# A mixture-of-experts encoder layer: sixteen short expert turns instead of fourteen, expert 0's rows by products, rank results by plain loads

## The chip, the core and the metric

The kernel runs on one core of a Trainium2 chip. The metric is the device time of one execution in microseconds, as the median of several runs; a profiled execution gives the trace. TensorE (PE) multiplies, with its own weight loads (PEld); VectorE (DVE), ScalarE (ACT) and GpSimd (POOL) work on tiles in SBUF; SyncE (SP) only issues transfers here. Sixteen DMA engines move the data, for the queues of SP (q1) and POOL (q0) alike.

## The reference, cut

One layer over 512 tokens of width 1024: attention, a LayerNorm, then a routed mixture of experts and a last LayerNorm. All numbers are float32.

```python
h = layer_norm(DN_ALPHA * h + mix, ln1_g, ln1_b)          # after two attentions and their projections
logits = t @ w_router + b_router                          # t: 512 x 1024, 32 experts
top_v, top_i = lax.top_k(logits, 4)
top_w = softmax(top_v)
# every expert takes the tokens that chose it (2048 token-expert pairs in all):
g = minimum(xb @ w_gate[e] + b_gate[e], 7)                # w_gate[e], w_up[e], w_down[e]: 1024 x 1024
u = clip(xb @ w_up[e] + b_up[e], -7, 7)
ys = (g * sigmoid(1.702 * g) * (u + 1)) @ w_down[e] + b_down[e]
out = segment_sum(ys * row_w, row_tok)                    # the four results of a token, weighted and added
h = layer_norm(DN_ALPHA * h + out, ln2_g, ln2_b)
```

An expert's three matrices are 12 MB; all 32 experts' are 384 MB, and each is read once.

## The kernel before, in words

**Stages.** First come the LayerNorm, both attentions and the output projection. They end in the loop over four token tiles `t` in which `mix`, `norm`, `z_turn`, `route` and `places` work out the normed rows, the four experts of each token and its place in each expert's list (`posp`). The scaled rows (`affine`) go to DRAM as `h1d`. Then 32 turns follow, one expert each.

**Turns.** Experts 0 and 1 are turns 0 and 1, whatever their number of tokens. The other 30 are sorted by that number: `count`, a comparison of all counts (`cmp_`, `rank`), a one-hot matrix `atT`, and in `turns_known` the list `turnI`, from which SyncE reads the expert of each turn before it loads the turn's weights. The smallest go to the turns with `SMALL[e]`, which have 64 places (turns 2, 4, ..., 28: fourteen); the others have 128. If an expert has more tokens than its turn has places, the rest is done in a loop behind the program (`n_over`), which is skipped otherwise.

- A turn of 128 places (`products`) multiplies in fp32r: each half megabyte of weights is split by ACT (`wh`, L88) and VectorE (`wl`, L89), and `mm3` (L158) makes three products of it.
- A turn of 64 places (`products64`, L1046) multiplies in fp32 with the weights as they come, 64 columns of PE for each half of the matrix; nothing is split.

**Rows of an expert.** POOL (for experts 0 and 1 VectorE, in `places`) makes `hots`, a one-hot matrix of a token tile against the places. `choose` multiplies it with `aux` on PE, which gives each place's token, weight and rank, as `tokI`, `wgt` and `dstI`. `gather` fetches the rows from `h1d` by an indirect DMA, and `x_turn` transposes them into `XT`. For experts 0 and 1 an early `choose` gives the tokens alone (`tok0`).

**The order of the turns** is written out by hand, and each engine runs its instructions in that order: `gates_of(f)`, `ups_of(f)`, then the down products of `e = f - 1`. The functions in the tables `at` are put in front of the half megabyte with that number (0 to 7) of a product.

**Loads.** `Stream` holds a list of chunks of 1 MB and a list of slots, 14 in the expert stage. A chunk is loaded by SyncE as soon as a slot is free, in the order of the list: for each turn four chunks of gate, four of up and four of down of the turn before. A slot comes free when its chunk has been split (128 places) or multiplied (64 places).

**Results.** A result row is written to `Y` in DRAM by an indirect DMA, to the place (rank of the expert among the token's four, token). Turns 30 and 31 don't write: `last_result` keeps their results as two parts, and `last_add` adds them per token tile by products with one-hot matrices (`last_turn`) into PSUM (`lastP`). `acc` holds the residual rows. After turn 29, twelve DMAs of POOL's queue add ranks 0 to 2 of `Y` to `acc` while they move (`add_rank`, L1151); the last four follow after VectorE has added `lastP`. Then ln2's rows are loaded, and VectorE, ACT and POOL make the last LayerNorm (`row_stats`, `ln_scale`, `ln2_norm`, `ln2_affine`).

Of the kernel before, what the change touches and what calls it, by code (L numbers as in the profile page):

```python
# [37 lines left out]
C_ID, C_IE, C_KB, C_RK, C_CAP, C_P, C_PM, C_IH, C_END = 0, 128, 160, 192, 224, 256, 257, 259, 260  # L38


SMALL = {e: 2 <= e < NE - 2 and e % 2 == 0 for e in range(NE)} | {"o": False}
# [3 lines left out]
class Stream:  # L45
# [3 lines left out]
    def __init__(self, nc, look):  # L49
        self.nc, self.look = nc, look  # L50
        self.free, self.chunks, self.halves, self.live = [], [], [], {}
        self.loaded = self.split = 0
        self.limit, self.low, self.queue = 1 << 30, nc.vector, nc.sync

# [3 lines left out]
    def add(self, shape, load, halves):  # L58

        first = len(self.halves)  # L60
        self.chunks.append([shape, load, None, None])
        for n, (view, make) in enumerate(halves):
            self.halves.append((len(self.chunks) - 1, view, make, n == len(halves) - 1))
# [50 lines left out]
def hybrid_attention_moe(ctx: ExitStack, tc: tile.TileContext, x, ln0_g, ln0_b, w_in, a_sink, b_q_norm, b_k_norm,  # L114
# [94 lines left out]
    def expert_at(e):  # L209

        if e < 2:
# [6 lines left out]
    def expert_chunks(w, e):  # L218

        r = []  # L220
        for c in range(4):
            def load(raw, c=c):
                v = w[0, ds(expert_at(e), 1)]
                if SMALL[e]:
                    v = v[:, c // 2 * 512:c // 2 * 512 + 512].rearrange("a (p b) f -> (a p) b f", b=4)
                    v = v[:, c % 2 * 2:c % 2 * 2 + 2]
                else:
                    v = v.rearrange("a (p j) f -> (a p) j f", j=8)[:, 2 * c:2 * c + 2]
                st.queue.dma_start(raw, v)
            r += st.add((2, DM), load, [(lambda q, i=i: q[:, i:i + 1], None if SMALL[e] else hl((1, DM)))  # L230
                                        for i in range(2)])
# [58 lines left out]
    cols = hd.tile([128, 4, 8], F32, name="cols")  # L290
    st.low = nc.gpsimd
    for t0 in (0, 2):
# [8 lines left out]
        if t0 == 0:  # L301
            p = ps.tile([128, 32], F32, name="pp", bufs=2)
            nc.tensor.transpose(p, rows, ident[:32, :32])
            nc.vector.tensor_copy(cols, p.rearrange("p (a b) -> p a b", b=8))
    st.limit = h_av[1]
# [200 lines left out]

    Y = dram.tile([4 * T, DM], F32, name="Y")
# [262 lines left out]
    def places(t):  # L770
# [4 lines left out]
        for e in range(2):  # L775
            find(hots[e], posp[:, :, e], [t], nc.vector)
# [32 lines left out]
    hots = {e: hots_of(None, n=e) for e in range(2)}  # L809
# [12 lines left out]
    selectors(iota_e, 0, 2)  # L822
# [40 lines left out]
    route(2)  # L863
    affine(3)
    z_turn(3)
    places(2)
    route(3)
    places(3)
    st.limit = 1 << 30

    close(ps, hd)
# [3 lines left out]
    mp = pool("mp")  # L875
    ps = pool("pm", space=PSUM)
# [23 lines left out]
    tok0 = ax.tile([128, 2], I32, name="tok0")  # L900
# [5 lines left out]
    def choose(e0, n, early=False):  # L906

        c = 2 if early else 6
# [5 lines left out]
        if early:  # L914
            tokens_of(tok0[:, e0:e0 + n], q)
# [522 lines left out]
```

## Time and profile before

| | |
|---|---|
| median of three runs | 1503.54 us (1502.82 to 1511.2) |
| the profiled execution | 1502.89 us, span 1501.1 us |
| PE, busy | 1394.7 us, 93% of the span |
| VectorE, ACT, POOL, busy | 945.5, 765.9 and 252.7 us |
| DMA | 469.69 MB, 313 GB/s over the span |
| granted TensorE clock, mean | 0.972 |

Times in rows are microseconds from the start of the span. The busy slices cut the span in 40 parts, each digit tenths of a slice. PEclk is the granted share of TensorE's clock; the five engines of a stretch are PE, PEld, DVE, ACT and POOL. In a timeline, consecutive instructions of one kind are one row with their count, and a bracket gives the idle time before and what ended it. `L` numbers are lines of the kernel.

### The profile page before, as it was taken

Reading aid. Unit: us, or ns where it says so; the run is one execution under the profiler, and the core shown is the slowest. Engines: PE = TensorE matmul, PEld = TensorE weight load, DVE = VectorE, ACT = ScalarE, POOL = GpSimd, SP = SyncE. Lnnn points to the kernel's source line nnn. Section 1 sums busy time; section 2 is a strip of 40 time slices with the busy share of each in tenths; the row PEclk is TensorE's granted clock in tenths of the full one; section 3 lists DMA queues with packets and bytes.
Section 4 is the critical chain, followed back from the end, with each engine's and each line's share of the span. In section 5 each row is a group of like instructions: output and inputs, shape, how many; then the busy total and the mean of one; then the engine's idle time right before and its main releaser. Section 6 shows DMA issues by size and latency. Waiting matters only on the chain.

```text
span 1501.1 us, 19430 instructions
## 1 busy us (share of the span) xinstructions
PE 1394.7 (93%) x6885; PEld 967.1 (64%) x6885; DVE 945.5 (63%) x1444; ACT 765.9 (51%) x1064; POOL 252.7 (17%) x295
## 2 busy tenths in 40 slices
PE   5999999999679999999799999999999999999990
PEld 3778877888557656475555756657566474667870
DVE  6675666464779548384754845747446383567986
ACT  4555556542357546264354635636446273556861
POOL 2000430101540210102021011110210101110113
PEclk9999999999799999999899999999999999999995
DMA  7362210326278999999899999999999999999996
GB/s 233 119 246 66 68 45 30 96 88 280 87 264 302 396 411 420 395 415 395 334 405 420 419 420 418 420 420 417 418 414 414 408 416 411 414 414 408 409 204 156
DMA packets 90023, 469.69 MB, mean 313 GB/s; under 512 B 10738, under 2 KB 29346, under 8 KB 40769
## 3 DMA queue, kind: packets, MB, share of 16 engines
q1 hardware_dynamic: 75888, 426.80, 70.9%
q0 software_dynamic: 13680, 41.45, 8.9%
q8 instruction: 56, 0.92, 0.2%
q14 instruction: 47, 0.38, 0.1%
q10 hardware_dynamic: 352, 0.15, 0.0%
HBM read 452.76 MB, written 24.64 MB: 318 GB/s over the span
## 4 chain that ended last, share of the span: by engine, by line
PE 41%; DMA 24%; DVE 5%; ACT 1%; issue 1%; POOL 1%; SPq 0%; ACTq 0%; DVEq 0%; POOLq 0%
PE d L158 9%; DMA raw<-in_w_down_dram 9%; PE g L158 8%; DMA raw<-in_w_gate_dram 8%; PE u L158 7%; PE g L1046 4%; PE u L1046 4%; PE d L1046 4%; DMA acc<-Y 3%; DMA raw<-in_w_up_dram 3%; DVE wl L89 2%; PE t L937 2%; ACT wh L88 1%; DMA Y<-y,dstI 1%; PE t L1108 1%
## 5 line engine op out<-in xcount | busy, mean ns | idle before, releaser
L89 DVE TENSOR_TENSOR wl<-raw,wh 128x1024 fp32r<-128x1024 f32 x472 | 565.3, 1227 | 122.9 <-ACT wh L88 108.9
L88 ACT ACTIVATE wh<-raw 128x1024 fp32r<-128x1024 f32 x476 | 494.6, 1057 | 183.7 <-PE d L158 63.7
L929 POOL DMA_INDIRECT xg<-h1d,tokI x30 | 42.6, 1421 | 729.2 <-PE t L1108 359.5
L153 DVE TENSOR_TENSOR atl<-t,ath 128x512 fp32r<-128x512 f32 x34 | 23.5, 690 | 178.3 <-ACT ath L152 178.0
L158 PE MATMUL d<-wh,ath 128*128 128x512 f32 x272 | 111.8, 411 | 7.2 <-ACT wh L88 7.2
L158 PE MATMUL u<-wl,xth 128*128 128x512 f32 x272 | 107.6, 395 | 8.1 <-DVE wl L89 8.1
L158 PE MATMUL g<-wh,xth 128*128 128x512 f32 x288 | 114.7, 398 | 0.0
L158 PE MATMUL d<-wl,ath 128*128 128x512 f32 x272 | 108.0, 397 | 6.8 <-DVE wl L89 6.6
L158 PE MATMUL g<-wh,xtl 128*128 128x512 f32 x288 | 112.7, 391 | 0.0
L158 PE MATMUL g<-wl,xth 128*128 128x512 f32 x288 | 112.6, 391 | 0.0
L158 PE MATMUL u<-wh,xth 128*128 128x512 f32 x272 | 108.2, 398 | 0.0
L158 PE MATMUL u<-wh,xtl 128*128 128x512 f32 x272 | 107.5, 395 | 0.0
L158 PE MATMUL d<-wh,atl 128*128 128x512 f32 x272 | 107.3, 394 | 0.0
L1046 PE MATMUL g<-raw,xth 128*64 128x512 f32 x448 | 105.4, 602 | 0.0
L1046 PE MATMUL u<-raw,xth 128*64 128x512 f32 x448 | 103.9, 600 | 0.7 <-DMA raw<-in_w_up_dram 0.7
L1046 PE MATMUL d<-raw,ath 128*64 128x512 f32 x448 | 102.8, 600 | 0.0
L158 PEld LDWEIGHTS d<-wh,ath 128*128 128x128 f32 x272 | 51.5, 189 | 28.1 <-ACT wh L88 12.4
L158 PE MATMUL pp<-hTH,wh 128*128 128x512 f32 x160 | 64.9, 406 | 0.0
L158 PEld LDWEIGHTS d<-wl,ath 128*128 128x128 f32 x272 | 51.7, 190 | 20.5 <-DVE wl L89 11.3
L1046 PEld LDWEIGHTS d<-raw,ath 128*64 128x64 f32 x448 | 29.7, 137 | 54.6 <-issue 47.9
L158 PEld LDWEIGHTS u<-wl,xth 128*128 128x128 f32 x272 | 51.9, 191 | 19.4 <-DVE wl L89 8.5
L1046 PEld LDWEIGHTS u<-raw,xth 128*64 128x64 f32 x448 | 29.0, 136 | 54.0 <-issue 47.5
(408 smaller groups left out, 2394.3 us busy)
## 6 DMA issues: line engine op xcount, KB each, us to landing
raw<-in_w_gate_dram SPq DMA_DIRECT2D x128, 1024.0 KB
raw<-in_w_down_dram SPq DMA_DIRECT2D x128, 1024.0 KB
raw<-in_w_up_dram SPq DMA_DIRECT2D x125, 1024.0 KB
raw<-in_w_in_dram SPq DMA_DIRECT2D x14, 1024.0 KB
Y<-u POOLq DMA_DIRECT2D x4, 2048.0 KB, 17.2
acc<-Y POOLq DMA_DIRECT2D x16, 512.0 KB, 10.0
raw<-in_w_out_dram SPq DMA_DIRECT2D x4, 1024.0 KB
raw<-in_w_up_dram POOLq DMA_DIRECT2D x3, 1024.0 KB, 7.6
```

Source lines behind the costliest of these rows:

```text
L88: self.nc.scalar.activation(h, src, AF.Copy)
L89: self.low.tensor_tensor(l, src, h.bitcast(F32), op=OP.subtract)
L153: nc.vector.tensor_tensor(l, src, h.bitcast(F32), op=OP.subtract)
L158: nc.tensor.matmul(o, a, b, start=start and i == 0, stop=stop and i == 2, **kw)
L929: nc.gpsimd.indirect_dma_start(out=x_[:, :T] if small else x_, out_offset=None, in_=src, in_offset=bass.IndirectOffsetOnAxis(ap=tok, axis= ...
L937: nc.tensor.transpose(p[:, j], src[:, 4 * i + j::8], ident)
L1046: nc.tensor.matmul(o[64 * i:64 * i + 64], xt(j), w[:, 0, i * 512:i * 512 + 512], start=j == 0 and sel is None, stop=j == 7, skip_group_che ...
L1108: nc.tensor.transpose(p[:, b], src[:, b:T:4], ident)
```

## The change

- **Turns.** Sixteen turns have 64 places: 1, 2, 4, ..., 24, 27, 30 and 31. Only expert 0 has a fixed turn; the other 31 are sorted.
- **Expert 0's rows** are not gathered. `pick` multiplies the normed rows of each token tile with expert 0's one-hot matrix (`hot0`) into PSUM as soon as the tile's places are known; ACT and VectorE scale the result with ln1's values (`cols1`), and it is split into `XT[0]`. Expert 0's gate and up chunks are laid out to fit. `hots` of experts 0 and 1 are now made by POOL, from the places by turn, and turn 1's rows are gathered in `first_rows`.
- **Loads.** Expert 0's down chunks stand before expert 1's gate chunks in the list. As turn 1 has an expert that is not known beforehand, `Stream.known` holds the loads there until `turns_known`. Behind the last weights come one chunk with ln2's rows and eight chunks of `Y`, two token tiles of one rank each.
- **Results.** No DMA adds in the regular program. `add_chunk` takes a chunk of `Y`, and VectorE adds its two tiles to `acc`. Turns 30 and 31 have one result tile each; `last_add` makes one fp32 product for each token tile and half.

The diff, cut:

```diff
-SMALL = {e: 2 <= e < NE - 2 and e % 2 == 0 for e in range(NE)} | {"o": False}
+SMALL = {e: e in (1, 27, 30, 31) or 2 <= e <= 24 and e % 2 == 0 for e in range(NE)} | {"o": False}
...
-        while self.loaded < len(self.chunks) and self.free:
+        while self.loaded < min(len(self.chunks), self.known) and self.free:
...
-        if e < 2:
+        if e == 0:
             return e
...
+                elif e == 0 and w is not w_down:
+                    v = v.rearrange("a (j p) f -> p (a j) f", p=128)[:, 2 * c:2 * c + 2]
...
         if e < NE:
+            if e == 1:
+                down0 = len(st.chunks)
+                expert_chunks(w_down, 0, ahead=True)
+                st.known = len(st.chunks)
             HG[e] = expert_chunks(w_gate, e)
             HU[e] = expert_chunks(w_up, e)
         if e > 0:
-            HD_[e - 1] = expert_chunks(w_down, e - 1)
+            HD_[e - 1] = expert_chunks(w_down, e - 1, behind=down0 if e == 1 else None)
+    def load_gb(raw):
+        for i, v in enumerate((ln2_g, ln2_b)):
+            nc.sync.dma_start(raw[:, i], v.to_broadcast([128, DM]))
+
+    def load_rank(r, q):
+        src = Y[r * T + q * 256:r * T + q * 256 + 256].rearrange("(a p) d -> p a d", p=128)
+        return lambda raw: nc.sync.dma_start(raw, src)
+
+    h_g2 = st.add((2, DM), load_gb, [(lambda q: q, None)])[0]
+    h_rank = {(r, q): st.add((2, DM), load_rank(r, q), [(lambda v: v, None)])[0] for q in range(2) for r in range(4)}
...
-        for e in range(2):
-            find(hots[e], posp[:, :, e], [t], nc.vector)
+        nc.vector.tensor_scalar(hot0[:, t], cnt1, posp[:, t, 0:1], None, op0=OP.is_equal)
+
+    def pick(t, first, last):
+
+        for k in range(KT):
+            nc.tensor.matmul(zp[k // 4][:, k % 4], z[t][k // 4][:, k % 4 * 128:k % 4 * 128 + 128], hot0[:, t],
+                             start=first and k % 4 == 0, stop=last, skip_group_check=True)
...
     route(2)
+    zp = [ps.tile([128, 4, 128], F32, name="s", bufs=3) for _ in range(2)]
+    pick(0, True, False)
+    pick(1, False, False)
     affine(3)
     z_turn(3)
     places(2)
+    pick(2, False, False)
     route(3)
     places(3)
+    pick(3, False, True)
...
+    XT = {0: turned("xth", "xtl")}
+    for i in range(2):
+        f = mp.tile([128, T], F32, name="rT").rearrange("p (a b) -> p a b", a=4)
+        for j in range(4):
+            g, b = (cols1[:, c, 4 * i + j:4 * i + j + 1] for c in range(2))
+            if j % 2:
+                nc.vector.tensor_scalar(f[:, j], zp[i][:, j], g, b, op0=OP.mult, op1=OP.add)
+            else:
+                nc.scalar.activation(f[:, j], zp[i][:, j], AF.Identity, bias=b, scale=g)
+        split_to(XT[0][0][:, 4 * i:4 * i + 4], XT[0][1][:, 4 * i:4 * i + 4], f)
...
-    choose(0, 1, True)
-    gather(xg, tok0[:, 0:1])
     st.queue = nc.gpsimd
     st.slots(mp, 3)
     st.load()
     st.queue = nc.sync
-    choose(1, 1, True)
...
-        selectors(turns, 2, NE)
+        selectors(turns, 1, NE)
+        st.known = 1 << 30
+        st.load()
...
+    def add_chunk(r, q):
+
+        v = st.get(h_rank[r, q])
+        for t in (2 * q, 2 * q + 1):
+            nc.vector.tensor_tensor(acc[:, t], acc[:, t], v[:, t % 2], op=OP.add)
+        st.done(h_rank[r, q])
...
     def last_result(e):
-        y = lastY[e] = slot(F32R)
-        w = wgt[:, e:e + 1]
-        for i in range(2):
-            s = slice(i * 512, i * 512 + 512)
-            nc.scalar.activation(y[:, 0, s], PD[e][i], AF.Copy, scale=w)
-            nc.vector.scalar_tensor_tensor(y[:, 1, s], PD[e][i], w, y[:, 0, s].bitcast(F32), op0=OP.mult,
-                                           op1=OP.subtract)
+        lastY[e] = mp.tile([128, T], F32, name="y" if e % 2 else "sg")
+        nc.scalar.activation(lastY[e], PD[e], AF.Copy, scale=wgt[:, e:e + 1])
...
+            s = slice(64 * i, 64 * i + 64)
+            nc.tensor.matmul(lastP[t, i], lastT[e % 2][s, t], lastY[e][s], start=e == NE - 2, stop=stop)
...
-    gates_of(0, {1: [turns_known], 2: [places_by_turn], 3: [weights_by_turn], 4: [parts_by_turn],
-                 5: [lambda: choose(0, 2), lambda: start(2, 1)]})
-    ups_of(0, {1: [lambda: choose(2, 1)], 2: [lambda: start(3, 2)], 4: [lambda: choose(3, 2)], 5: [lambda: x_turn(1, 0)], 6: [lambda: x_turn(1, 1)]})
+    def first_rows():
+        choose(0, 2)
+        gather(xg, tokI[:, 1:2], SMALL[1])
+        start(2, 1)
+
+    gates_of(0, {1: [turns_known], 2: [places_by_turn], 3: [lambda: start(0, 2), weights_by_turn], 4: [parts_by_turn],
+                 6: [first_rows]})
+    ups_of(0, {1: [lambda: choose(2, 1)], 2: [lambda: start(3, 2)], 4: [lambda: choose(3, 2)], 6: [lambda: x_turn(1, 0)]})
...
             if e == NE - 2:
-                at = {5: [lambda: a_turn(f, 0)], 6: [lambda: a_turn(f, 1)]}
+                at = {3: [lambda: add_chunk(0, 0)], 5: [lambda: a_turn(f, 0)], 6: [lambda: add_chunk(1, 0)]}
             if e >= NE - 3:
                 at[2] = [lambda: last_turn(f)]
         else:
-            at = {j + 3: [lambda t=j: last_add(e - 1, t)] for j in range(3)}
+            at = {2 * j + 1: [lambda t=j: last_add(e - 1, t)] for j in range(3)}
+            for j, c in enumerate(((2, 0), (3, 0), (0, 1), (1, 1))):
+                at[2 * j] = [lambda c=c: add_chunk(*c)]
...
-        if e == NE - 3:
-            for r in range(3):
-                for t in range(NT):
-                    add_rank(r, t, Y)
-
-    last_result(NE - 1)
+    add_chunk(2, 1)
+    add_chunk(3, 1)
+    gb = st.get(h_g2)
...
         for i in range(2):
             a = two(acc[:, t])[i]
             nc.vector.tensor_tensor(a, a, lastP[t, i], op=OP.add)
-        add_rank(3, t, Y)
-    for i, v in enumerate((ln2_g, ln2_b)):
-        nc.gpsimd.dma_start(gb[:, i], v.to_broadcast([128, DM]))
```

## Rows read from the trace of the kernel before

**Rows 1.** The page: busy slices, and median landing times of DMA issues.

```profile
DMA  7362210326278999999899999999999999999996
...
raw<-in_w_up_dram POOLq DMA_DIRECT2D x3, 1024.0 KB, 7.6
```

**Rows 2.** Stretches: us, five engines' busy time (count), PEclk, DMA share, GB/s.

```profile
457.00:900.00 443.00, 434.10 (x1967) 270.31 (x1966) 276.15 (x341) 225.92 (x264) 64.88 (x84) 0.99 0.98 397
...
900.00:1410.00 510.00, 495.91 (x2263) 317.14 (x2262) 310.46 (x348) 271.72 (x316) 70.29 (x84) 1.00 1.01 415
...
720.00:750.00 30.00, 21.90 (x86) 14.70 (x85) 21.72 (x40) 9.05 (x11) 0.00 (x0) 0.83 0.78 311
...
302.00:306.00 4.00, 4.00 (x19) 3.22 (x18) 2.12 (x3) 0.93 (x2) 0.00 (x0) 1.00 0.80 262
...
342.00:350.00 8.00, 8.00 (x36) 6.52 (x35) 2.08 (x3) 2.75 (x3) 0.00 (x0) 1.00 1.01 424
...
1440.00:1480.00 40.00, 26.38 (x116) 20.61 (x114) 28.15 (x42) 16.26 (x22) 9.70 (x12) 0.87 0.97 195
```

**Rows 3.** The chain that ended last: start us, us, what.

```profile
805.49 4.44 PE d L1046 x20
...
813.76 4.44 PE g L1046 x20
...
822.79 3.58 PE u L1046 x16
...
830.24 7.04 PE d L158 x30
...
865.60 4.44 PE d L1046 x20
...
962.35 21.69 DMA raw<-in_w_gate_dram
...
1304.70 21.68 DMA raw<-in_w_down_dram
...
1471.88 8.54 DMA acc<-Y
```

**Rows 4.** Timeline of the SyncE queue: start us, us, line, operation, count.

```profile
462.87 9.04 SPq L229 DMA_DIRECT2D raw<-in_w_up_dram  x4
...
1401.28 19.12 SPq L229 DMA_DIRECT2D raw<-in_w_down_dram  x8
```

**Rows 5.** Timelines of PE, VectorE and POOL around turn 0.

```profile
399.16 1.11 PE L740 MATMUL pp<-con,ga 128*128 128x128 f32 x4 [2.17 <-ACT ga L731]
...
416.92 0.63 PE L158 MATMUL g<-wh,xth 128*128 128x512 f32 x1
...
455.40 0.40 PE L1061 MATMUL g<-bgu,es 128*128 128x512 f32 x1
...
413.85 0.29 DVE L997 TENSOR_TENSOR lh<-lh,ew 128x128 f32<-128x128 f32 x1
...
420.80 0.17 DVE L1004 CAST turnI<-turns 1x32 int32<-1x32 f32 x1
...
433.30 5.70 POOL L768 TENSOR_SCALAR hots<-to,posp 128x128 bf16<-128x128 bf16 x4 [15.28 <-PE t L881]
...
442.30 4.92 POOL L768 TENSOR_SCALAR hots<-to,posp 128x128 bf16<-128x128 bf16 x4
```

**Rows 6.** Timeline of VectorE in the tail.

```profile
1470.30 1.28 DVE L1305 TENSOR_TENSOR acc<-acc,g 128x512 f32<-128x512 f32 x2 [1.20 <-DMA acc<-Y]
...
1480.44 1.29 DVE L267 BATCH_NORM_STATS2 bst<-acc 128x6 f32<-128x512 f32 x2 [0.84 <-DMA acc<-Y]
...
1481.76 0.21 DVE L268 BATCH_NORM_AGGREGATE mv<-bst 128x2 f32<-128x12 f32 x1
...
1483.31 7.96 DVE L1294 TENSOR_TENSOR raw<-raw,raw 128x512 f32<-128x512 f32 x6
```

**Rows 7.** Costliest groups: count, busy us, mean ns, idle before.

```profile
L89 DVE TENSOR_TENSOR wl<-raw,wh 128x1024 fp32r<-128x1024 f32 x472 | 565.3, 1227 | 122.9 <-ACT wh L88 108.9
```

More of the change, by code (lines that the diff above doesn't have):

```diff
@@ L53, in __init__ @@
         self.limit, self.low, self.queue = 1 << 30, nc.vector, nc.sync
+        self.known = 1 << 30
     def slots(self, pool, n):
@@ L216, in expert_at, with expert_chunks @@
         return turn_regs[e]
-    def expert_chunks(w, e):
+    def expert_chunks(w, e, ahead=False, behind=None):
         r = []
@@ L229, in load @@
                 st.queue.dma_start(raw, v)
-            r += st.add((2, DM), load, [(lambda q, i=i: q[:, i:i + 1], None if SMALL[e] else hl((1, DM)))
-                                        for i in range(2)])
+            halves = [(lambda q, i=i: q[:, i:i + 1], None if SMALL[e] else hl((1, DM))) for i in range(2)]
+            if behind is not None:
+                r += st.use(behind + c, halves)
+            else:
+                r += st.add((2, DM), load, [] if ahead else halves)
         return r
@@ L290, in hybrid_attention_moe @@
     cols = hd.tile([128, 4, 8], F32, name="cols")
+    cols1 = keep.tile([128, 2, 8], F32, name="cols1")
     st.low = nc.gpsimd
@@ L807, in hots_of @@
         return d
-    hots = {e: hots_of(None, n=e) for e in range(2)}
+    hots = {}
+    hot0 = hd.tile([128, NT, 128], F32, name="PT", bufs=2)
     bgu = rp.tile([128, 2, T], F32R, name="bgu")
@@ L820, in selectors @@
                                     op0=OP.is_equal)
-    selectors(iota_e, 0, 2)
+    selectors(iota_e, 0, 1)
     raws = []
@@ L904, in start, with choose @@
             hots[e] = hots_of(posp[:, :, e], nc.gpsimd, e, small=SMALL[e])
-    def choose(e0, n, early=False):
-        c = 2 if early else 6
+    def choose(e0, n):
+        c = 6
         p = ps.tile([128, 2, 8], F32, name="t", bufs=2)
@@ L913, in choose @@
         nc.vector.tensor_copy(q, p[:, :n, :c])
-        if early:
-            tokens_of(tok0[:, e0:e0 + n], q)
-            return
         tokens_of(tokI[:, e0:e0 + n], q)
@@ L938, in turn @@
         split_to(h[:, 4 * i:4 * i + 4], l[:, 4 * i:4 * i + 4], p)
-    def turned(*names):
-        return [mp.tile([128, 8, 128], F32R, name=n) for n in names]
-    choose(0, 1, True)
-    gather(xg, tok0[:, 0:1])
     st.queue = nc.gpsimd
@@ L1157, in last_turn @@
         if not lastT:
-            d = mp.tile([128, 2, NT, 128], F32R, name="bd")
+            d = mp.tile([128, 2, NT, 128], F32, name="bd")
             lastT.update({i: d[:, i] for i in range(2)})
@@ L1180, in last_add @@
             if e == NE - 2:
-                n, b = (("u", 0), ("d", 0), ("t", 2), ("g", 0))[t]
-                lastP[t, i] = ps.tile([128, T], F32, name=n if b else f"{n}{i}", bufs=b or 1)
-            s = slice(i * 512, i * 512 + 512)
-            for j in range(2):
-                nc.tensor.matmul(lastP[t, i], lastT[e % 2][:, t], lastY[e][:, j, s], start=e == NE - 2 and j == 0,
-                                 stop=stop and j == 1)
+                n, b = ((("u0", 1), ("u1", 1)), (("d0", 1), ("d1", 1)), (("t", 2), ("t", 2)), (("g1", 1), ("g0", 1)))[t][i]
+                lastP[t, i] = ps.tile([128, T], F32, name=n, bufs=b)
+            s = slice(64 * i, 64 * i + 64)
+            nc.tensor.matmul(lastP[t, i], lastT[e % 2][s, t], lastY[e][s], start=e == NE - 2, stop=stop)
     eb = ax.tile([128, 3, NB + 1], F32, name="eb")
@@ L1408, in _tables @@
     c[:, C_CAP:C_CAP + NE] = CAP
-    c[:, C_KB:C_KB + NE] = np.arange(NE) + np.where(np.arange(NE) < 2, 1e5 * (1 + np.arange(NE)), 0.0)
-    turns = [e for e in range(2, NE) if SMALL[e]] + [e for e in range(2, NE) if not SMALL[e]] + [0, 1]
+    c[:, C_PH] = i % 64 + 1
+    c[:, C_KB:C_KB + NE] = np.arange(NE) + np.where(np.arange(NE) < 1, 1e5, 0.0)
+    turns = [e for e in range(1, NE) if SMALL[e]] + [e for e in range(1, NE) if not SMALL[e]] + [0]
     c[:, C_RK + np.array(turns)] = np.arange(NE)
```

51 lines of the change are left out of this document (27 added, 24 removed).

## The prediction, made before the result was known

> **What bounds the kernel now.** I read the busy slices of the page first, then stretches of the span, then the chain of waits, then the SyncE timeline. In the slices the DMA engines are full from about a third of the span to the end of the expert turns [rows 1]. The stretches say the same in bytes: 415 GB/s at a share of 1.01 between 900 and 1410 us, but only 397 GB/s between 457 and 900 [rows 2]. PE looks full in both, and that misleads: in the first half a pair of turns (one of 128 places, one of 64) takes 865.60 - 805.49 = 60.1 us of matmuls back to back, while further on the chain consists of weight loads [rows 3]. There the first gate megabyte of turn 18 was issued at 962.35 and landed 21.69 us later, at 984.04; the first down megabyte of turn 27 landed at 1304.70 + 21.68 = 1326.38. A turn loads 12 MB in the order gate, up, down of the turn before; counted from 0, gates of turn 2 begin with number 20, so the two are numbers 20 + 12 x 16 = 212 and 20 + 12 x 26 + 8 = 340: 342.3/128 = 2.675 us a megabyte, 32.1 us a turn, 64.2 us a pair. PE (60.1) is faster than that. A load waits 21.7 us for 2.675 us of work, so some eight are in flight. The weight stream is the bound; PE sets the pace only while the loader has no free slot. After the weights, the chain runs through the accumulating DMAs of the rank results, until the last one lands at 1471.88 + 8.54 = 1480.4 [rows 3], and then a VectorE tail.
>
> So I price the change as a stream: when it becomes full, how many megabytes it still has, and what follows the last one.
>
> **Two more turns of 64 places, by themselves.** They take PE time away (a turn of 64 places: gates 813.76 to 822.79, up to 830.24, and a down of the 813.76 - 805.49 kind [rows 3], 24.7 us in all, which leaves 35.4 for the other sort) but not one byte: both sorts load 12 MB. In a stretch bound by loads this is worth nothing, and it spares ACT and VectorE the splits that lie beside them. It counts where PE sets the pace, which is early.
>
> **The early part.** The first up megabyte of turn 2, number 24 counted from 0, is issued at 462.87 [rows 4]. Loads issued into a nearly empty queue on POOL landed after 7.6 us by the median of three [rows 1], and those did meet each other; I take 6, so 469. To number 212, 188 MB at 2.675 would be 502.9 us; they took 984.0 - 469 = 515. So 12 us of loading time are lost in between. Counted in bytes it is more, 443 x (1 - 397/415) = 19 us, 7.5 of them in the one stretch 720 to 750 at 311 GB/s [rows 2], where the VectorE block of `blocks` holds up the splits. I take 12, as it is counted in landed megabytes, and keep 19 as the other end.
>
> In the changed kernel turns 1 and 2 both have 64 places. Such a turn gives a slot back every 9.03/4 = 2.26 us, faster than 2.675, so from turn 1 on the loader always has a slot and the stream is full. Its start hangs on the end of turn 0.
>
> Turn 0, step by step. Expert 0's rows no longer wait for a gather. Thirty-two small fp32 products are added; the nearest row is of transposes of the same tile, four in 1.11 us [rows 5], 0.28 each, so the sixteen of `pick(0)` and `pick(1)` are 4.5 us, or 2.2 at half that price, of which 2.17 fall into PE's idle time before 399.16. They delay the last token tile by 0 to 2.3 us; I take 1. After that, eight scalings and two splits of 128x512 give XT[0] some 3 us before the 416.92 of now. This is not kept: the count and rank chain of VectorE, which now ends at 413.85 + 0.29 [rows 5], stands behind those splits and ends near 419; two weight splits follow it, so `turnI` comes near 422 instead of 420.97. PE waits for that chain in `turns_known`. Then `hots` of experts 0 and 1, made by VectorE before, are made by POOL behind the places by turn (four take some 5 us: 433.30 for 5.70, 442.30 for 4.92), then the gather of turn 1, which waits for its indices, then `hots` of 2, 3 and 4. PE waits for each in `choose`. I put gates of turn 1 at 458 instead of 455.40 [rows 5]; the ends are 452 (`hots` at half of those 5 us, no delay by `pick`) and 464 (all at 5.7, `pick` at its dear end).
>
> By the end of turn 0's up, 14 slots plus 8 returned ones have let 22 MB out, as before; number 22 goes out with the first slot of turn 1 at 460.3, lands about 5 us later, and number 24 lands near 470.6, so 1.6 us later than now. The first down matrix, loaded early, fills slots that waited for the turn order; loads of expert 1 now wait for `turnI`, and those waits are covered by gates and up of turn 0, which are at hand: were that cover gone (`turnI` some 15 us late), the stream would start late by the excess. `blocks` still stops the splits, for some 12 us, but about one more load is in flight then; I leave 1 us of the 7.5. The stream is thus 12 - 1.6 - 1 = 9.4 us ahead by turn 18, with ends 3 and 19.
>
> **The last turns.** From there on the pace is the same. The first of the last eight down loads, number 376, goes out at 1401.28 [rows 4]; with eight in flight number 368 has just landed. In the changed kernel that is 1391.9, and 15 MB remain: 15 x 2.675 = 40.1, so the weights are in at 1432.0. Two long turns in a row, twice near the end, put PE 2 x (35.4 - 32.1) = 6.6 us behind, 2.5 of the 14 slots: the loader keeps going. The short turns 30 and 31 give that back, so PE ends some 3 us after the last weight. The scatter of turn 29 must land before SyncE may issue the first rank chunk; it stands behind nothing but other rank chunks there, and eight loads are in flight to cover it.
>
> **The rank chunks.** Sixteen accumulating DMAs go; 1 MB of ln2 rows and eight 1 MB chunks come behind the weights on SyncE's queue. No row shows Y read plainly. Ends: 2.5 us a megabyte, as weights of 8 KB pieces before the turns (424 GB/s, 342 to 350), and 5.2, as the accumulating reads (195 GB/s, 1440 to 1480). The nearest row is w_out between 302 and 306, which has the same 4 KB rows, two to a partition, from the same queue: 262 GB/s at a share of 0.80, 327 GB/s when full, 3.2 us a megabyte [rows 2]. Nine chunks take 28.8 us (ends 22.5 and 47): the last is in at 1460.8. VectorE's two adds of each (1.23 each [rows 7]) keep up with 3.2, and nothing PE needs stands behind them. The Trainium skill (DMA: Bandwidth & Descriptors, Why small descriptors are slow) gives a fixed 3 cycles per packet beside 32-byte beats, by which 4 KB and 8 KB packets differ by 1% (my estimate from that page). Here the row disagrees (3.2 against 2.5); by that rule the sum would be some 6 us smaller.
>
> **The tail.** What is late next is VectorE, in order: two adds of the last chunk, 2 x 1.23; four pairs of adds from PSUM, 4 x 1.28 (they now stand between products and accumulating DMAs, and move behind the last chunk); four rows of statistics, 4 x (1.29 + 0.21); two chains of small operations, 2 x 1.34; and from the first affine multiply to the end 1501.1 - 1483.31 = 17.8 [rows 6, 7]. That is 34.1 us after the last chunk, against 20.7 after the last accumulating DMA now. The ln2 loads leave the tail; they were hidden there. End: 1494.9 of span. The profiled run was 1.8 us over its span and the median is 0.65 over the profiled run: 1497.
>
> **Rivals.** (1) *The stream recovers all of it and the chunks are cheap.* 19 instead of 12 recovered, turn 0 at 455, chunks at 2.5: 1497 - 7 - 3 - 6 = 1481; half of these, 1485. For it: the byte count. Against: w_out's row. (2) *Rank chunks cost what accumulating ones cost*, 5.2 us: 1497 + 18 = 1515, slower than before. The place is after the last weight, and it decides from 3.9 us a chunk on, (28.8 + 6.2)/9. For it: the memory read is Y, whose rows are slow now. Against: there the DMA engine also adds. (3) *Turn 0 late*: 464 or more, 1503. (4) *The change does not do what it says*: by the reference's inputs the sixteenth smallest of experts 1 to 31 has 63 tokens, under the 64 places, so no overflow block runs; if one did, another 12 MB at least, over 1529.
>
> **How the numbers follow.** Forecast (1490 to 1502) 0.55; rival 1 0.22; rival 2 0.13; rival 3 0.08; rival 4 0.02. A change of 1% is about what this kernel's measurement can tell: below 1488.5 or above 1518.6. Rival 1 and a little of the forecast's edge give 0.2 for faster; the upper end of rival 2 and rival 4 give 0.06 for slower; 0.74 in between. For 8 in 10 the range takes in most of rivals 1 and 2: 1482 to 1512.
>
> **What would show it.** The DMA share should be at 1.01 from about 460 on, 720 to 750 included; the last weight near 1432; nine chunks in about 29 us; 34 us from the last landing to the end; PE idle for the last 55 us or more. I am wrong if PE's products still end last, if the stretch 457 to 900 stays near 397 GB/s, or if a chunk takes 2.5 or over 4 us.

## The result: 1495.4 us, and the profile after

The changed kernel takes 1495.37 us (median of 6 runs, 1493.19 to 1496.93), the kernel before 1503.38 (6 runs beside them): a ratio of 0.993, 95% interval 0.9907 to 0.9952. The forecast was 1497.0. The profiled execution took 1494.61 us, its span 1492.8. TensorE's mean granted clock is 0.972 in both. So the total came out 1.6 us from the forecast; its terms did not, and two of them were wrong in opposite directions.

The busy slices and the landing times of the page, which answer to [rows 1]:

```profile
DMA  7362110227248999999899999999999999999981
...
raw<-Y SPq DMA_DIRECT2D x8, 1024.0 KB, 17.5
```

The DMA engines are full nearly to the end of the rank chunks, then almost idle for the tail. The same stretches as in [rows 2], with the same columns:

```profile
457.00:900.00 443.00, 435.09 (x1952) 256.48 (x1952) 252.91 (x320) 206.59 (x245) 67.82 (x85) 0.99 0.99 405
900.00:1410.00 510.00, 505.40 (x2291) 322.96 (x2289) 318.04 (x353) 277.61 (x322) 81.37 (x84) 1.00 1.01 415
720.00:750.00 30.00, 22.09 (x89) 13.14 (x89) 18.61 (x38) 6.87 (x9) 1.03 (x1) 0.89 0.85 336
```

Between 457 and 900 there are 405 GB/s now, 397 before; the later stretch is unchanged at 415. The hole at 720 to 750 is smaller, 336 instead of 311, but it is still there. The chain that ended last, for [rows 3]:

```profile
932.09 4.44 PE g L1095 x20
...
992.98 4.44 PE g L1095 x20
...
1108.36 21.73 DMA raw<-in_w_down_dram
...
1402.43 21.05 DMA raw<-in_w_down_dram
...
1443.80 14.91 DMA raw<-Y
```

A pair of turns is 60.9 us of PE. The two down loads are numbers 268 and 378 counted from 0: 294.07/110 = 2.673 us a megabyte, the forecast's 2.675. Now SyncE's timeline, for [rows 4]:

```profile
468.42 6.86 SPq L237 DMA_DIRECT2D raw<-in_w_up_dram  x4
...
520.46 9.74 SPq L237 DMA_DIRECT2D raw<-in_w_up_dram  x4
...
1397.48 18.97 SPq L237 DMA_DIRECT2D raw<-in_w_down_dram  x8
...
1423.55 20.66 SPq L265 DMA_DIRECT2D raw<-Y  x8
```

Number 24 goes out at 468.42, 5.55 us later than before. Number 48 goes out at 520.46. In the kernel before that was

```profile
526.56 3.05 SPq L229 DMA_DIRECT2D raw<-in_w_up_dram  x2
```

so these 24 loads were issued in 52.0 us instead of 63.7: 11.6 us are won here. The lead does not grow from there. It is 6.1 us at number 48, falls to 2.7 at number 180, and then stands between 2.6 and 4.7 (4.35 at number 212, 3.8 at number 376). It is a lead of issues, not of bytes; the bytes are won more slowly, part of them between 600 and 720, where the kernel before moved 403 GB/s and this one 413. Rank chunks 1 to 6 each wait for a weight (378 to 383) to land, 2.47 us apart, so the last weight is in near 1423.55 + 5 x 2.47 = 1435.9. The last chunk lands at 1443.80 + 14.91 = 1458.7: nine chunks in 22.8 us, 2.53 each. From there to the end of the span are 34.1 us.

Around turn 0, for [rows 5], PE first, then VectorE:

```profile
401.25 1.16 PE L810 MATMUL s<-PT,ga 128*128 128x128 f32 x8 [2.48 <-DVE PT L805]
...
403.57 3.46 PE L777 MATMUL pp<-tab,kp 128*128 128x32 f32 x16
...
461.89 0.40 PE L1093 MATMUL g<-bgu,bd 128*128 128x512 f32 x1
```

```profile
407.07 0.19 DVE L778 TENSOR_TENSOR lh<-pp,cb 128x32 f32<-128x32 f32 x1 [5.87 <-PE pp L777]
...
412.65 0.41 DVE L928 TENSOR_SCALAR rT<-s,cols 128x128 f32<-128x128 f32 x1 [2.66 <-ACT rT L930]
...
418.63 0.18 DVE L1012 COPY cnt<-t 128x32 f32<-128x32 f32 x1
...
426.47 0.17 DVE L1051 CAST turnI<-turns 1x32 int32<-1x32 f32 x1
```

PE takes `pick(2)` (L810) before `route(3)` (L777), and the pick waits 2.48 us for its one-hot tile; VectorE idles 5.87 us for the route. Then VectorE's scalings of XT[0] (L928) wait for ACT's in turn, and the count chain starts at 418.63 behind them. `turnI` comes 5.67 us later than in [rows 5], and gates of turn 1 start at 461.89 instead of 455.40. VectorE in the tail, for [rows 6]:

```profile
1440.96 2.36 DVE L1206 TENSOR_TENSOR acc<-acc,raw 128x1024 f32<-128x1024 f32 x2 [16.85 <-DMA raw<-Y]
...
1458.81 2.36 DVE L1206 TENSOR_TENSOR acc<-acc,raw 128x1024 f32<-128x1024 f32 x2 [0.17 <-DMA raw<-Y]
1461.08 1.28 DVE L1358 TENSOR_TENSOR acc<-acc,u 128x512 f32<-128x512 f32 x2
...
1465.87 1.27 DVE L297 BATCH_NORM_STATS2 bst<-acc 128x6 f32<-128x512 f32 x2
...
1474.38 7.96 DVE L1347 TENSOR_TENSOR raw<-raw,raw 128x512 f32<-128x512 f32 x6
...
1483.93 0.68 DVE L1347 TENSOR_TENSOR raw<-raw,raw 128x512 f32<-128x512 f32 x1
```

From the first chunk on VectorE hardly stops: it waits some 0.2 us for each chunk and nothing after the last.

### The profile page after: what moved, and what is told of

It reads as the page before. It is cut to its first block, busy times and chain, and to the rows that moved or that the text cites. A ratio compares the mean times of both kernels' runs of the same rounds, so it can differ in the third digit from the quotient of the medians.

```text
span 1492.8 us, 19169 instructions
## 1 busy us (share of the span) xinstructions
PE 1384.7 (93%) x6817; PEld 926.5 (62%) x6817; DVE 898.1 (60%) x1395; ACT 715.7 (48%) x1014; POOL 250.6 (17%) x281
## 4 chain that ended last, share of the span: by engine, by line
PE 69%; DMA 18%; DVE 9%; ACT 2%; issue 1%; POOL 1%; SPq 0%; ACTq 0%; DVEq 0%; POOLq 0%
PE g L163 10%; PE u L163 9%; PE d L163 8%; DMA raw<-in_w_down_dram 7%; PE pp L163 7%; PE g L1095 5%; PE u L1095 5%; PE d L1095 5%; DMA raw<-in_w_up_dram 4%; DMA raw<-in_w_gate_dram 4%; PE s L163 4%; DMA raw<-Y 2%; PE pt L453 2%; PE o L465 2%; PE t L990 2%; PE pt L163 2%
## 5 line engine op out<-in xcount | busy, mean ns | idle before, releaser
L94 DVE TENSOR_TENSOR wl<-raw,wh 128x1024 fp32r<-128x1024 f32 x424 | 509.0, 1227 | 117.2 <-ACT wh L93 112.8
L93 ACT ACTIVATE wh<-raw 128x1024 fp32r<-128x1024 f32 x428 | 444.7, 1056 | 168.1 <-PE d L163 72.6
L982 POOL DMA_INDIRECT xg<-h1d,tokI x31 | 45.3, 1463 | 718.4 <-PE t L1157 362.2
L1095 PE MATMUL g<-raw,xth 128*64 128x512 f32 x512 | 120.2, 601 | 0.0
L1095 PE MATMUL d<-raw,ath 128*64 128x512 f32 x480 | 110.4, 599 | 0.0
L163 PE MATMUL g<-wh,xth 128*128 128x512 f32 x256 | 104.3, 407 | 0.9 <-ACT xth L157 0.9
L163 PE MATMUL g<-wh,xtl 128*128 128x512 f32 x256 | 102.4, 400 | 0.0
L163 PE MATMUL g<-wl,xth 128*128 128x512 f32 x256 | 102.4, 400 | 0.0
L1126 DVE TENSOR_SCALAR u<-u 128x512 f32<-128x512 f32 x48 | 33.4, 695 | 64.0 <-PE u L163 38.3
L1095 PEld LDWEIGHTS g<-raw,xth 128*64 128x64 f32 x512 | 32.7, 136 | 56.6 <-issue 50.0
L163 PE MATMUL pp<-hTL,wh 128*128 128x512 f32 x160 | 63.9, 399 | 0.0
```

What stands on the lines that cost most here:

```text
L93: self.nc.scalar.activation(h, src, AF.Copy)
L94: self.low.tensor_tensor(l, src, h.bitcast(F32), op=OP.subtract)
L163: nc.tensor.matmul(o, a, b, start=start and i == 0, stop=stop and i == 2, **kw)
L982: nc.gpsimd.indirect_dma_start(out=x_[:, :T] if small else x_, out_offset=None, in_=src, in_offset=bass.IndirectOffsetOnAxis(ap=tok, axis= ...
L1095: nc.tensor.matmul(o[64 * i:64 * i + 64], xt(j), w[:, 0, i * 512:i * 512 + 512], start=j == 0 and sel is None, stop=j == 7, skip_group_che ...
L1126: nc.vector.tensor_scalar(u, u, -6.0, 8.0, op0=OP.max, op1=OP.min)
```

## The experiments

The theory, called S in the expectations: the end is the moment at which the weight stream becomes full, plus its megabytes, plus what stops it, plus what follows. All times are medians and all edits are made on the changed kernel (1495.4) unless told otherwise. Positions in single traces carry an error of their own: in the eight kernels below that change nothing before number 24 it stands between 467.32 (e4) and 471.56 (e3), and `turnI` between 424.4 and 429.7. So a single position there is good to some 2 us, and shifts of the start are read from the medians first. Stretches behind number 24 are steadier: from number 24 to number 376 the changed kernel and the six below that change nothing in between (e1, e2, e3, e7, e8, e10) take 929.1 to 929.8 us, the kernel before 938.4.

**e1, expert 0's rows gathered again.**

```diff
...
-    pick(0, True, False)
-    pick(1, False, False)
...
-    pick(3, False, True)
...
+    choose(0, 1, True)
+    gather(xg, tokI[:, 0:1])
...
+    for i in range(2):
+        x_turn(0, i)
...
```

> Undoes one part of the change: expert 0's rows are gathered from h1d again (early choice of their tokens, gather, transposes), everything else stays. Theory S (the end is the moment at which the weight stream becomes full, plus its megabytes, plus what stops it, plus the tail): route of the last token tile and the count chain of VectorE no longer stand behind the products of pick and the scalings of XT[0], so turnI should come near 418 to 420 instead of 426.47, number 24 be issued some 4 to 7 us before 468.42, and the end follow one to one: 1488 to 1491 against 1495.4 of the changed kernel. Rival L (number 24 came 5.5 us late in the changed kernel and number 48 was nevertheless 6.1 us ahead, so turn 0's start doesn't pass on): the end stays at 1495 within 1.5 us. Rival W (XT[0] waits for its gather, 1 MB class DMAs of POOL in front of it): turn 0 starts later than now and the end goes to 1497 or more.

Measured 1487.33 us (1486.53 to 1488.77), 8.0 less than the changed kernel. VectorE and SyncE in its trace:

```profile
403.45 0.19 DVE L776 TENSOR_TENSOR lh<-pp,cb 128x32 f32<-128x32 f32 x1 [1.06 <-PE pp L775]
...
418.94 0.17 DVE L1032 CAST turnI<-turns 1x32 int32<-1x32 f32 x1
```

```profile
460.65 6.86 SPq L235 DMA_DIRECT2D raw<-in_w_up_dram  x4
```

`turnI` is 7.5 us earlier, number 24 is 7.8 us earlier, the end 8.0, a little more than S had said (1488 to 1491). S holds, L and W fall: the shift of the start reaches the end one to one, as far as the positions can tell. This part of the change costs 8 us.

**e2, only `pick(2)` moved.**

```diff
-    pick(2, False, False)
     route(3)
+    pick(2, False, False)
```

> One line is moved: pick of token tile 2 goes behind route of tile 3, so that its products don't stand in front of route's on PE. In the changed kernel pick(2) waits 2.48 us for its one-hot tile and takes 2.5 us, and VectorE then idles 5.87 us for route(3). Theory S: route(3) reaches VectorE near 403 instead of 407.07, turnI near 422.5 instead of 426.47, number 24 is issued some 4 us earlier, the end is some 4 us earlier: 1491.5. Rival L: the end stays at 1495 within 1.5 us although turnI is earlier.

Measured 1491.52 (1488.62 to 1502.19), 3.9 less. The trace has `turnI` at

```profile
422.98 0.17 DVE L1051 CAST turnI<-turns 1x32 int32<-1x32 f32 x1
```

3.5 us earlier, and number 24 at 464.12, 4.3 earlier; both lie outside the spread given above. As S had it: half of the 8 us is one `pick`'s products in front of one `route`'s on PE. The other half of e1's gain is then the rest of `pick`, the scalings and the other layout of expert 0's gate and up chunks; no run parts these.

**e3, the accumulating DMAs again.** Twelve `add_rank` behind turn 29, four behind the adds of `lastP`, ln2's rows by POOL at the end; no rank chunks.

```diff
-    h_g2 = st.add((2, DM), load_gb, [(lambda q: q, None)])[0]
-    h_rank = {(r, q): st.add((2, DM), load_rank(r, q), [(lambda v: v, None)])[0] for q in range(2) for r in range(4)}
...
+        if e == NE - 3:
+            for r in range(3):
+                for t in range(NT):
+                    add_rank(r, t, Y)
...
```

> Undoes one part of the change: the rank results are added by sixteen accumulating DMAs of POOL's queue again and ln2's rows are loaded at the end by POOL; turns and expert 0's rows stay as changed. Theory S: the weights are issued as now (number 383 at 1416), and from there the end takes as long as in the kernel before: last accumulating DMA lands near 1476.4 (1480.4 less the 4.0 us that number 383 is earlier), 20.7 us of tail, span 1497, time 1499: 3.5 us slower than the changed kernel, which would be the whole worth of the plain chunks. Rival C (the chunks save much more, as the accumulating DMAs also slow the last weights): 1503 or more. Rival N (the chunks save nothing, their gain is eaten by the longer tail): 1495 within 1.5 us.

Measured 1500.21 (1497.25 to 1502.76), 4.8 more. Its SyncE row and the end of its chain:

```profile
1401.36 18.94 SPq L237 DMA_DIRECT2D raw<-in_w_down_dram  x8
```

```profile
1471.38 8.39 DMA acc<-Y
```

From the first of the last eight down loads to the end of the span it takes 1500.1 - 1401.36 = 98.7 us, against 1492.8 - 1397.48 = 95.3 with chunks: 3.4 us is what the chunks are worth in the traces, 4.8 in the medians. S named 3.5; C and N fall.

**e8, the chunk with ln2's rows behind the rank chunks.**

```diff
-    h_g2 = st.add((2, DM), load_gb, [(lambda q: q, None)])[0]
     h_rank = {(r, q): st.add((2, DM), load_rank(r, q), [(lambda v: v, None)])[0] for q in range(2) for r in range(4)}
+    h_g2 = st.add((2, DM), load_gb, [(lambda q: q, None)])[0]
```

> The chunk with ln2's rows is loaded behind the eight rank chunks instead of in front of them, all else as in the changed kernel. Theory C (a chunk costs 2.53 us, (1458.7 - 1435.9)/9, and the nine follow one another): each rank chunk lands one chunk earlier, the last at 1456.2, ln2's rows at 1458.7, well before the affine step at 1474; the end is 2.5 us earlier, 1492.9. Rival V (VectorE's adds, 2.36 us a chunk, pace the chunks, or ln2's rows, 4 KB for all partitions, cost less than a chunk): less than 1 us of gain.

Measured 1492.56 (1491.19 to 1499.99), 2.8 less. The last rank chunk in its chain

```profile
1440.79 15.36 DMA raw<-Y
```

lands at 1456.15, 2.55 before the 1458.7 of the changed kernel, with number 376 issued at 1397.48 in both. The ranges overlap, so the medians alone would not settle it; with the trace C holds: a chunk costs 2.5 us, ln2's rows too.

**e12, turn 1 with 128 places.**

```diff
-SMALL = {e: e in (1, 27, 30, 31) or 2 <= e <= 24 and e % 2 == 0 for e in range(NE)} | {"o": False}
+SMALL = {e: e in (27, 30, 31) or 2 <= e <= 24 and e % 2 == 0 for e in range(NE)} | {"o": False}
...
```

(Its rows are transposed in two steps, in front of the up halves 5 and 6 of turn 0, as in the kernel before.)

> Turn 1 has 128 places, as in the kernel before, all else as in the changed kernel (fifteen short turns; its rows are transposed in two steps, in front of the up halves 5 and 6 of turn 0). Theory S1 (what the change wins in the expert stage is won by turn 1: with a short turn 1 the loads number 24 to 48 were issued in 52.0 us instead of 63.7): number 48 is issued some 11 us after 520.46, nothing of it comes back, the end is at 1504 to 1507. Rival D (PE's debt after a long turn 1 is paid back at 3.2 us a pair before `blocks`, and the stream only sees part of it): 1497 to 1500. Rival N (a turn's length costs nothing, as I had put it for the two more short turns): 1495 within 1.5 us.

Measured 1508.39 (1506.83 to 1516.2), 13.0 more than the changed kernel and more than the kernel before. Its SyncE rows for numbers 24 and 48:

```profile
468.97 8.93 SPq L237 DMA_DIRECT2D raw<-in_w_up_dram  x4
...
533.29 9.74 SPq L237 DMA_DIRECT2D raw<-in_w_up_dram  x4
```

64.3 us for the 24 loads, as in the kernel before (63.7), where the changed kernel takes 52.0; and nothing of it comes back. S1's mechanism holds, with an end 1.4 us above its range; D and N fall. What the change wins in the expert turns lies in this one. The parts also add up: the kernel before, plus the 8.0 of `pick`, less the 4.8 of the chunks is 1506.6, near the 1508.4 of this run.

**e4, turns 14 and 20 with 128 places.**

```diff
-SMALL = {e: e in (1, 27, 30, 31) or 2 <= e <= 24 and e % 2 == 0 for e in range(NE)} | {"o": False}
+SMALL = {e: e in (1, 27, 30, 31) or 2 <= e <= 24 and e % 2 == 0 and e not in (14, 20) for e in range(NE)} | {"o": False}
```

> Fourteen turns of 64 places instead of sixteen: turns 14 and 20 get 128 places again, all else stays as changed. Theory S (a stretch bound by loads doesn't see PE's time): 264 weight loads from number 120 to 383 take 703 us as now within 2 us, the end is at 1495 within 2 us, though PE has 21 us more work. It holds while PE is not further behind than the slots cover (14 slots less 8 in flight, 6 x 2.67 = 16 us). Rival P (PE's chain is what counts, as the chain of waits shows PE from 802 to 1096): the end is later by 10.7 to 21 us, 1506 to 1517.

Measured 1503.33 (1501.12 to 1509.67), 8.0 more: S's number fell, and P's too. What SyncE waits for between 1100 and 1410, this kernel:

```profile
SPq L237 <- DVE wl L94: 168.2, 72, 4.7
SPq L237 <- PE g L1095: 35.3, 16, 4.6
```

and the changed kernel, from 457 to 1100:

```profile
SPq L237 <- DVE wl L94: 167.7, 80, 11.9
SPq L237 <- PE d L1095: 67.1, 34, 5.8
SPq L237 <- PE g L1095: 64.7, 37, 6.6
SPq L237 <- PE u L1095: 30.5, 21, 2.8
```

The changed kernel's loader waits for slots in the first half, 330 us in these four rows; after 1100 it waits for landings almost alone. With 14 and 20 long it waits for slots to the end, and for 2.1 us more until turn 29's results have landed, before the first rank chunk. The new theory D: PE is in debt (behind the loads) when the stream starts, as all slots are filled; it pays 3.3 us back in each pair (64.2 - 60.9), and only what exceeds the slots' cover costs time.

**e6, turn 22 with 128 places.**

```diff
-SMALL = {e: e in (1, 27, 30, 31) or 2 <= e <= 24 and e % 2 == 0 for e in range(NE)} | {"o": False}
+SMALL = {e: e in (1, 27, 30, 31) or 2 <= e <= 24 and e % 2 == 0 and e != 22 for e in range(NE)} | {"o": False}
```

> Turn 22 gets 128 places, fifteen short turns are left. Fourteen with 14 and 20 long cost 8 us. Theory D (a debt of PE: PE comes behind by 3.3 us in a long turn, catches up 7.4 in a short one, and the stream only loses what goes beyond some 16 us of free slots): at turn 22 PE has caught up (from about 1100 on SyncE waits for no slot), the extra 10.7 us are covered, the end stays at 1495 within 1.5 us. Rival P (each turn that is lengthened costs the same, wherever it stands): half of the 8 us, 1499.

Measured 1496.22 (1495.24 to 1500.82), 0.9 more, within the spread of both: by the median D holds and P falls, though the range takes in P's 1499. But e4 lengthened two turns and e6 one, so the medians alone don't tell the place from the amount. The traces help. In e4 turn 14 begins at 871 and turn 20 at 1067. Around turn 14, this is e4, then the changed kernel:

```profile
900.00:1000.00 100.00, 99.24 (x452) 71.16 (x453) 74.69 (x78) 63.52 (x73) 13.01 (x14) 1.00 0.99 396
```

```profile
900.00:1000.00 100.00, 100.00 (x453) 62.19 (x453) 56.44 (x61) 49.72 (x60) 17.20 (x23) 1.00 1.01 419
```

and here is e6, whose turn 22 begins at 1116, then the changed kernel:

```profile
1000.00:1410.00 410.00, 408.47 (x1860) 278.05 (x1857) 293.67 (x321) 251.62 (x288) 70.46 (x60) 1.00 1.01 410
```

```profile
1000.00:1410.00 410.00, 405.40 (x1840) 260.77 (x1836) 261.60 (x292) 227.89 (x263) 64.17 (x61) 1.00 1.01 413
```

Turn 14 alone costs the stream 5.5 us of loading, turn 22 costs it some 3, of which the median shows 0.9 at the end. So the place matters, but a late long turn is cheap rather than free; what turn 14 alone would cost at the end, no run shows.

**e5 and e9, `blocks` in turn 21, and in turn 15** (the diff is e5's; e9 has 15 there).

```diff
-            if f == 9:
+            if f == 21:
```

> One number is changed: the VectorE block of blocks() runs in turn 21 instead of turn 9, all else as in the changed kernel. Theory S: at 720 the loader waits for slots (SyncE waits 300 us for VectorE's splits and PE's products between 457 and 1100, and almost none after 1100), so a stop of the splits of some 12 us lets the DMA engines run dry: 336 GB/s in the stretch 720 to 750, 5.7 us lost. In turn 21, near 1120, the slots are mostly free and the stop is covered (6 slots x 2.67 = 16 us). The stretch 720 to 750 comes near 415 GB/s, number 376 is issued some 5 us before 1397.48, the end is near 1490. Rival G (the loader makes it up later anyway, since PE is then further ahead): the end stays at 1495 within 1.5 us. Rival E (PE, put 12 us behind in front of the long turns 25, 26, 28 and 29, ends last): 1498 or more.

> As the run with blocks() in turn 21, but in turn 15, near 920. There the time from 720 to 750 was won (419 GB/s) and half of it lost again: PE, stopped near 1100, stayed behind through the pairs of long turns 25, 26 and 28, 29. Theory D (debt): without blocks PE has caught up from 790 on (the chain consists of weight loads from there), a stop of 12 us near 920 is covered by the slots and paid back at 3.2 us a pair by 1165, before the long pairs; nothing is lost and the end is 5 to 6 us before that of the changed kernel: 1490. Rival K (a stop of the splits costs some 3 us wherever it stands, as the splits behind it are late too): 1492 to 1493, as in turn 21.

Measured 1492.75 (1490.99 to 1494.46) and 1494.2 (1490.23 to 1499.74): 2.6 and 1.2 less, with intervals that overlap the changed kernel's. In the traces the time from number 24 to number 376 is 2.3 and 2.5 us shorter. The stretches with turn 15:

```profile
720.00:750.00 30.00, 30.00 (x133) 15.92 (x133) 11.78 (x13) 10.02 (x15) 6.71 (x10) 1.00 1.01 419
900.00:950.00 50.00, 42.08 (x186) 21.81 (x185) 27.23 (x53) 16.02 (x20) 6.70 (x10) 0.93 0.97 392
457.00:900.00 443.00, 443.00 (x1998) 263.40 (x1998) 252.87 (x305) 213.68 (x253) 68.65 (x86) 1.00 1.00 411
900.00:1410.00 510.00, 499.45 (x2255) 318.43 (x2254) 320.89 (x375) 270.57 (x314) 79.97 (x83) 0.99 1.01 412
```

The hole at 720 is gone, but a smaller one stands where the block is now: 411 instead of 405 up to 900 are 6.4 us won, 412 instead of 415 after it 3.7 lost. My S for turn 21 and D for turn 15 promised all of it; K, some 3 us wherever it stands, is nearer. Its reason is not the whole one: with turn 21 part of the gain is lost before the block is reached, as here, where the changed kernel has 419:

```profile
900.00:1000.00 100.00, 100.00 (x459) 58.03 (x459) 51.01 (x65) 44.34 (x54) 16.23 (x22) 1.00 1.01 412
```

What the loss hangs on stays open, and a block cut in pieces was not tried.

**e7 and e10, the tail parted in two ways.** Both also give POOL's affine steps to VectorE. First (e7): PE adds one token tile of each chunk to `lastP`, VectorE the other, and rows 0 and 1 (token tiles 0 and 1) are normed before the chunks of rows 2 and 3.

```diff
...
+            nc.tensor.matmul(lastP[t + 1, i], ident, v[:, 1, i * 512:i * 512 + 512], start=False, stop=r == 3)
...
```

> The work behind the rank chunks is parted otherwise: PE adds one of the two tiles of each chunk to lastP by a product with the identity, VectorE the other; rows 0 and 1 get their sums, statistics and norm before the chunks of rows 2 and 3; all affine steps are VectorE's. Theory V (from the first rank chunk at 1440.96 on VectorE is what ends last, 44 us of its work in 46): half of the chunk adds (9.8 us) leave it, and of the rest 7 us move ahead of the last landing, the end comes 10 to 14 us earlier, 1481 to 1485. Rival K (PE's clock: granted 0.83 between 1440 and 1456, after it went idle; a 128x512 product in fp32 is some 0.85 us at full clock and twice that at half, 16 of them 14 to 27 us): PE ends behind the last chunk and the gain is 0 to 7 us, 1488 to 1495.

Measured 1488.08 (1484.48 to 1490.96), 7.3 less. PE's granted clock was 1.00 between 1440 and 1456, so K's reason did not come true; VectorE remained the bound. The gain is K's upper end, less than V promised. Second (e10): VectorE keeps the chunks of rows 0 and 1 and finishes these rows while PE adds all of rows 2 and 3, residual rows too, by `add_rows` (products with `ident` into `lastP`).

```diff
...
+            if q:
+                add_rows(t, v[:, t % 2], r == 3)
+            else:
+                nc.vector.tensor_tensor(acc[:, t], acc[:, t], v[:, t % 2], op=OP.add)
...
```

> A second way to part the tail: VectorE adds the chunks of rows 0 and 1 and finishes these rows while PE adds all of rows 2 and 3 (residual rows and four ranks) to lastP by products with the identity; statistics and norm of rows 2 and 3 are read from PSUM. In the first way PE took 0.89 us a product at full clock and VectorE stayed the bound, without a gap from 1452 to 1482. Theory V: after the last landing at 1458.7 PE ends at 1465.4 (four chunks of 3.56 from 1451), then 3.0 of statistics, 1.3 of chain, 5.5 of affine steps for two rows and 6.3 to the end: 1481.5 of span, 11 us less than the changed kernel, 1484 (the first way gave 1488.1). Rival K (PE waits for chunks between its products and its clock falls to half): PE ends 7 us later, 1491.

Measured 1483.1 (1481.0 to 1486.27), 12.3 less. PE's last products, and VectorE's next step:

```profile
1463.93 1.88 PE L1214 MATMUL t<-raw,con 128*128 128x512 f32 x4
1465.65 1.88 PE L1214 MATMUL g<-raw,con 128*128 128x512 f32 x4
```

```profile
1466.26 1.29 DVE L297 BATCH_NORM_STATS2 bst<-t 128x6 f32<-128x512 f32 x2
```

PE ends at 1467.53, VectorE is free for the statistics of row 2 at 1466.26: both arrive close together, as V had worked out; K falls.

**e11, three at once:** expert 0's rows gathered, `blocks` in turn 15, the second tail.

> Three edits on the changed kernel at once: expert 0's rows gathered again, blocks() in turn 15, the second tail. Theory S says that they add, since one moves the start of the stream, one takes out a stop and one shortens what follows: 1495.4 - 8.1 - 5.5 - 11 = 1471. Rival M (they hide each other: an earlier stream meets PE's debt, so that the gains of the first two overlap): 1475 to 1480.

Measured 1472.65 (1471.01 to 1480.08), a ratio of 0.9777 to the kernel before, interval 0.9752 to 0.9802: it beats both kernels. The single gains, 8.0 + 1.2 + 12.3 = 21.5, add up to 1473.9. S holds (1471), M falls (1475 to 1480). The execution that was profiled took 1480.08 us and was late before the expert turns began, so no row of it is shown.

## Why the prediction was right, point by point

**The bound** was named rightly. The pace is 2.673 for 2.675, and both shifts of the start reached the end (e1, e2). But up to about 1100 PE sets the loader's pace beside it, as the point on the stream tells.

**Turn 0** was forecast to make number 24 late by 1.6 us and gates of turn 1 start at 458; it was 5.55 us and 461.89, near the upper end of 464 (by the spread of number 24 in the other kernels, 4.4 to 8.7 us). From `turnI` to these gates it took 35.4 us, forecast 36; the loss lies before `turnI`, which came at 426.47 instead of near 422. The step that failed is "They delay the last token tile by 0 to 2.3 us; I take 1", said of the sixteen products of `pick(0)` and `pick(1)`. These took 3.7 us, inside their 2.2 to 4.5. But I counted the two picks that stand before the last tile's transposes and passed over `pick(2)`, which stands in front of its route and waits for VectorE. Moving it gave 3.9 us back. The count chain I had rightly put behind the splits, but from an XT[0] 3 us earlier than before; ACT and VectorE alternated on one tile and waited for each other, and the chain began at 418.63, near where it was to end (419).

**The stream from turn 1 on.** Its origin was right: a short turn 1 lets the loader go on, and turn 1 alone is worth 13 us. "From turn 1 on the loader always has a slot" was wrong: it waits 330 us for slots up to 1100. With it fell "In a stretch bound by loads this is worth nothing": between 457 and 1100 the DMA engines are full and slots are short at the same time. Turns 14 and 20 short are worth 8 us at the end, turn 22 0.9. Of the 11 us that were to be won between number 24 and number 212 the trace has 11.6 by number 48, 9.9 at number 212 and 9.35 at number 376; no run takes the 2.3 us between the first and the last apart.

**`blocks`**: 1 us of 7.5 was to be left; (1 - 336/415) x 30 = 5.7 are. "About one more load is in flight then" was the failed step, as the loader waits for slots there. Moving the block (e5, e9) gave back less than half of it.

**The rank chunks**: forecast 28.8 us for nine, measured 22.8, the cheap end; a chunk of 2.53 is also what the prediction had named as a sign of being wrong. I had scaled a 4 us stretch in which w_out's queue was not full to a price per megabyte. In the changed kernel the same 4 us are

```profile
302.00:306.00 4.00, 4.00 (x18) 3.19 (x18) 1.35 (x3) 0.63 (x1) 0.00 (x0) 1.00 0.33 134
```

and the same scaling gives 406 GB/s (134/0.33) instead of 327: such an edge gives no price. VectorE kept up as forecast, with 2.36 us of adds for a chunk of 2.53.

The Trainium skill (DMA: Bandwidth & Descriptors, Why small descriptors are slow) states a fixed overhead of some 3 cycles for each packet; by my estimate from it 4 KB and 8 KB packets cost nearly the same. The trace agrees, with 2.53 here against the 2.5 of [rows 2]; the sum by that rule, 6 us smaller for this term, was the right one.

Rival 2 (5.2 us a chunk, accumulating prices) is excluded by these 2.53 and by e8.

**The tail**: 34.1 forecast, 34.1 measured; 16.3 were to go before the first affine multiply and 17.8 behind its start, and 15.7 and 18.4 did. PE was to be idle for the last 55 us; its last product ends at 1445.4, 47 us before the end, which cost nothing, as VectorE was still on the chunks.

**The other rivals**: of rival 1 the cheap chunks came true and the early turn 0 did not. Rival 3 (gates of turn 1 at 464 or more) was missed by 2 us. (Half of rival 1's 16 us would have made 1489, not 1485; that sum was wrong, and no reading hangs on it.) Rival 4 did not happen: no weights are loaded behind the 384 MB.

The account: number 24 is 3.95 us later than forecast, 1.65 less are won behind it, the last weights come 1.7 faster (2.47 us a load at the end), the chunks are 6.0 cheaper: 1494.9 + 3.95 + 1.65 - 1.7 - 6.0 = 1492.8, the span. That the total came so close is luck: the start and the chunks were wrong in opposite directions. The range, 1482 to 1512, held because it was wide: 452 to 464, and 2.5 to 5.2 a chunk, stood in it as bounds.

## What to carry to other kernels

Where a full load stream sets the end, look at what delays its start first: each microsecond there is one at the end, and a few small products in front of others on PE's queue, waiting for another engine, took 3.9 us where the whole change won 8.0. What a shorter turn is worth is read from what the loader waits for in that stretch, a slot or a landing, not from whether PE looks full. Price a new transfer from a stretch in which its queue was full, or not at all.

## What the hardware showed beside that

**The DMA engines don't end together.** The last 40 slices of 1 us each, from 1423 to 1463 of the changed kernel:

```profile
DMA  9889959999998998999967999995323211100000
GB/s 365 320 344 377 377 242 406 393 365 385 418 320 344 410 430 315 401 401 410 410 254 225 352 410 414 414 410 205 135 115 135 115 70 53 41 4 0 0 0 0
```

From 1450 on the share falls to 0.5 and then to 0.1, and only 0.87 MB move in the last nine microseconds, though chunks land every 2.5 us until 1458.7. That reads as a few engines that run behind the others, with each chunk waiting for the slowest; it was not tested.

**VectorE beside GpSimd.** The six multiplies at 1474.38 take 1.33 us each while POOL adds (8.26 us for five from 1475.20); the one at 1483.93, alone, takes 0.68. The Trainium skill (SBUF — State Buffer, SBUF: two separate sides) says that the two share a port pair as an exclusive lock, for VectorE instructions with two inputs in SBUF beside a GpSimd operation that reads SBUF; the trace agrees, and in the second tail, where VectorE has all the affine steps and POOL none, each takes 0.69 or less.

**PE as an adder.** A product of 128x512 with the identity in fp32 took 0.86 us (1.72 a pair, between the starts at 1463.93 and 1465.65) at a granted clock of 1.00, the upper of the two levels; between 1440 and 1456 the mean was 0.83 in the changed kernel, where PE ran out of work, and 1.00 in this one.
